# One PSUM bank set of five instead of 2 + 2 + 1 in a fused attention layer on one core

## Chip, cores and metric

The kernel runs on one core of a Trainium2 chip. The metric is the device time of one execution in microseconds (us). An execution of before takes 1867.32 us (median of three runs, 1866.57 to 1867.34).

## The reference

One encoder layer on x of shape (1, 2048, 1024), all float32: a modulated RMSNorm, one combined input projection, three groups of attention heads that share nothing but that projection, a gate for each, one output projection, a residual and a final RMSNorm. Cut to what matters:

```python
mod = c_act @ w_ada + b_ada
shift, scale, gate = jnp.split(mod, 3, axis=-1)
h = rmsnorm(x, norm_g) * (1.0 + scale[:, None, :]) + shift[:, None, :]
z = h @ w_in
...
a_out = mla_mixer(a_cq, a_ckv, a_kpe, ...)           # 6 heads, causal by chunks of 64
b_out = chunk_band_mixer(b_q, b_k, b_v, b_rel_bias)  # 5 heads, own chunk and 8 before, position bias
c_out = forgetting_mixer(c_q, c_k, c_v, c_f, ...)    # 5 heads, causal, cumulative log-forget bias
y = jnp.concatenate([a_out * silu(a_gate), b_out * silu(b_gate), c_out * silu(c_gate)], axis=-1) @ w_out
out = rmsnorm(x + gate[:, None, :] * y, final_g)
```

Each mixer is softmax(q k^T * scale + bias, masked) v for a head of 64 value columns.

## The kernel before

The 2048 tokens are worked off in two halves of 1024. Each half has a first stage (`stage_lv`: norm and transposition of x into `hT`, the latents of the A heads, the values of all heads, and the q and k of the first head) and then `attention()`, a loop over all 16 heads in a written order. In half 1 that order is B0 to B4, C0 to C4, A0 to A5. Every product of two float32 factors is made of three matmuls on rounded high and low parts (L359, L360, L361); a projection of one group of 128 columns for one block of 512 tokens is 24 such matmuls into one PSUM tile.

A head has two blocks of 512 queries, and a block is worked off in tiles of 128 keys by 512 queries, 580 score tiles in all. For a tile:
- TensorE makes the scores in a `st` tile (three or four matmuls, L982, L992 or L1050 to L1052).
- ScalarE takes exp of it three times (L755 into `ph`, L756 into `p32`, L758 in place), VectorE makes the low part `pl` (L764), GpSimd adds `p32` to the running sum (L769).
- Three tiles later TensorE adds the tile to `pv` by two matmuls (L778 with `ph`, L779 with `pl`).

At the end of a block ScalarE copies `pv` out (L784), GpSimd multiplies by the head's gate (L787, L788), and two tiles named `mx` turn the sums (L797, read by L798) and their reciprocals (L806, read by VectorE's L808, `oo`). Before a block can begin its queries need a row maximum: matmuls into `mx` tiles (L959, L970, L1040), reduced by VectorE (L962, L971, L1041), and a last turn by L722 to L723.

Between the tiles `step()` puts in a share of other work (`fill`): the projection of the next head's q and k into `pj` tiles (read by `evac`, ScalarE's L911, L912, L915, L916 and VectorE), the projections of the gates (G0 to G4, GA0 to GA2, read by ScalarE's L850 and VectorE's L851), and what the table `mids` lists by the head's number. In half 1 `mids[12]` loads the output weights (`load_wo`: DMA into one of three `wr` buffers, L1062; ScalarE's high part L1063; VectorE or GpSimd's low part L1064), `mids[13]` holds the last gate, GA2, and `mids[14]` and `mids[15]` the first eight of 16 output tiles (L1073 loads the heads' results into a `wr` buffer, L1076 and L1077 make `oh` and `ol`, then 48 matmuls into two `pj` tiles). The output weights `wo` take the one buffer of tag `big`, in which `hT` lies until its last reader, a matmul of GA2, has run.

PSUM has eight banks of 128 x 512 float32. Each PSUM tile is asked for by name through `pst(tag)`, and a tag has banks of its own: three for `st`, two for `mx`, two for `pj`, one for `pv`. Within a tag the banks are given out in the order in which the program asks. A tile that finds no free bank of its tag waits for the last reader of the oldest one. The order of the instructions on each engine is not that of the program text: a scheduler at build time places an instruction when its inputs and its buffer are free in its own reckoning, so the banks of a tag also set how far work may be placed ahead of its turn.

Of the kernel before, what the change touches and what calls it, by code (L numbers as in the profile page):

```python
# [8 lines left out]
F32 = mybir.dt.float32  # L9
# [52 lines left out]
def kernel(ctx: ExitStack, tc: tile.TileContext, a: dict, out: bass.AP):  # L62
# [8 lines left out]
    ps = ctx.enter_context(tc.tile_pool(name="ps", bufs=2, space=PSUM))  # L71
    dr = ctx.enter_context(tc.tile_pool(name="dr", bufs=1, space=DRAM))

    def pst(tag, bufs=2):
        return ps.tile([128, 512], F32, tag=tag, name=tag, bufs=bufs)

    def opool(name, bufs=2, side="left"):
        return tc.tile_pool(name=name, bufs=bufs, side=side, reuse_waits="tile")
# [100 lines left out]
    def h_units(hT, x_of, xn_of, tmp_of, ptag, norms=None):  # L179

        pairs = []
        for p2 in range(4):
            xns = []

            def norm(j, p2=p2, xns=xns):
                t = p2 * 2 + j
                xt, xn = x_of(t), xn_of()
                if norms is None:
                    r = col("xrr")
                    x_norm(xt, xn, r)  # L190
                else:
                    r = norms[:, t:t + 1]
                A.activation(xn, xt, AF.Copy, scale=r)
                xns.append(xn)

            def turn(k, p2=p2, xns=xns, box={}):
                o = 256 * (k % 2)
                if o == 0:
                    box["tp"] = pst(ptag, 3 if ptag == "st" else 2)
                tp = box["tp"][:, o:o + 256]  # L200
                for j in range(2):
                    T.transpose(tp[:, 128 * j:128 * j + 128], xns[j][:, 128 * k:128 * k + 128], ident)
                tmp = tmp_of(k)
                A.activation(tmp, tp, AF.Identity, scale=sc1[:, k:k + 1], bias=shf[:, k:k + 1])
                h = hT()
                hi = h[:, 0, k, 256 * p2:256 * p2 + 256]
                V.tensor_scalar(hi, tp, sc1[:, k:k + 1], shf[:, k:k + 1], op0=ALU.mult, op1=ALU.add)
                (V, G)[k % 2].tensor_tensor(h[:, 1, k, 256 * p2:256 * p2 + 256], tmp, hi.bitcast(F32), op=ALU.subtract)
            pairs.append([lambda j=j, f=norm: f(j) for j in range(2)] + [lambda k=k, f=turn: f(k) for k in range(8)])
# [12 lines left out]
    with opool("ada", 2, "right") as pool:  # L222

        mod = pst("mx")
        for c in range(2):
            acc = pool.tile([128, D], F32, tag="acc", name="acc")
            if c == 1:
                ident = load_const("ident", [128, 128])
                bada = load_const("b_ada", [128, 24])
                ng = load_const("norm_g", [128, 8])  # L230
                dma(out=posi, in_=a["positions"])
                dma(out=inv, in_=a["inv_freq"].to_broadcast([128, 16]))
                rotary(pool)
            for k in range(8):
                wa = pool.tile([128, D], F32, tag="wa", name="wa", bufs=8)
                dma(out=wa, in_=a["w_ada"][128 * k:128 * k + 128, D * c:D * c + D])
                if k == 0:
                    V.tensor_scalar(acc, wa, cact[:, 0:1], 0.0, op0=ALU.mult, op1=ALU.add)
                else:
                    V.scalar_tensor_tensor(acc, in0=wa, scalar=cact[:, k:k + 1], in1=acc, op0=ALU.mult, op1=ALU.add)  # L240
            for j in range(8):
                T.matmul(mod[:, 8 * c + j:8 * c + j + 1], lhsT=acc[:, 128 * j:128 * j + 128], rhs=ones[:, 0:1], start=True, stop=True)
        for u in h0[0][:2]:
            u()
        V.tensor_tensor(shf, mod[:, 0:8], bada[:, 0:8], op=ALU.add)
        V.tensor_tensor(sc1, mod[:, 8:16], bada[:, 8:16], op=ALU.add)
        V.scalar_tensor_tensor(sc1, in0=sc1, scalar=1.0, in1=ng, op0=ALU.add, op1=ALU.mult)
# [20 lines left out]
    def late_constants():  # L268
        tp = pst("mx")
        T.transpose(tp[:, 0:128], tri, ident)  # L270
        V.tensor_scalar(mtt, tp[:, 0:128], 1.0, BIG, op0=ALU.subtract, op1=ALU.mult)
# [1061 lines left out]
```

## Time and profile before

| what | value |
|---|---|
| median of three runs | 1867.32 us |
| the profiled execution, its own time | 1863.08 us |
| its span | 1861.1 us |
| mean granted TensorE clock | 0.983 of full speed |
| instructions | 28271 |
| TensorE busy | 1714.6 us (92%) |
| ScalarE busy | 1195.3 us (64%) |
| VectorE busy | 1132.8 us (61%) |
| GpSimd busy | 1071.9 us (58%) |

The profiled execution lies 4.2 us under the median of the runs, and its span 2.0 us under its own time. A busy time is the union of an engine's instructions; PE is the TensorE's matmuls, PEld its weight loads, DVE the VectorE, ACT the ScalarE, POOL GpSimd, SP the engine that issues the DMAs. A line as `PE pj L359 <- ACT q L916` reads: a matmul of line 359 into a tile named pj waited, and what came last was the ScalarE instruction of line 916 that writes q.

### The profile page before, as it was taken

Reading aid. Unit: us, or ns where it says so; the run is one execution under the profiler, and the core shown is the slowest. Engines: PE = TensorE matmul, PEld = TensorE weight load, DVE = VectorE, ACT = ScalarE, POOL = GpSimd, SP = SyncE. Lnnn points to the kernel's source line nnn. Section 1 sums busy time; section 2 is a strip of 40 time slices with the busy share of each in tenths; the row PEclk is TensorE's granted clock in tenths of the full one; section 3 lists DMA queues with packets and bytes.
Section 4 is the critical chain, followed back from the end, with each engine's and each line's share of the span. In section 5 each row is a group of like instructions: output and inputs, shape, how many; then the busy total and the mean of one; then the engine's idle time right before and its main releaser. Section 6 shows DMA issues by size and latency. Waiting matters only on the chain.

```text
span 1861.1 us, 28271 instructions
## 1 busy us (share of the span) xinstructions
PE 1714.6 (92%) x8835; PEld 1415.7 (76%) x8835; DVE 1132.8 (61%) x2447; ACT 1195.3 (64%) x2574; POOL 1071.9 (58%) x1256
## 2 busy tenths in 40 slices
PE   3899989999999986999899999999999997999997
PEld 2799868778777754999778887777777775877786
DVE  7453547866656587344456667777777776644322
ACT  3552347678768688342357778898998887665611
POOL 1541137568655557340156666777777778787864
PEclk9999989999999999999999999999999998999999
DMA  7514845435223241144933232222332334332243
GB/s 278 166 56 149 223 137 154 124 105 186 73 77 115 63 137 46 58 133 120 249 107 95 82 89 77 75 61 76 91 99 86 88 102 129 95 113 72 71 139 113
DMA packets 139994, 209.83 MB, mean 113 GB/s; under 512 B 18734, under 2 KB 72494, under 8 KB 139764
## 3 DMA queue, kind: packets, MB, share of 16 engines
q1 hardware_dynamic: 139844, 208.03, 37.2%
q8 instruction: 70, 1.15, 0.3%
q14 instruction: 80, 0.66, 0.1%
HBM read 154.05 MB, written 57.38 MB: 114 GB/s over the span
## 4 chain that ended last, share of the span: by engine, by line
PE 41%; ACT 7%; POOL 4%; issue 3%; DVE 3%; DMA 1%; SPq 0%; ACTq 0%; DVEq 0%; POOLq 0%
PE pj L359 5%; PE pj L360 5%; PE pj L361 5%; PE pv L778 3%; PE pv L779 3%; PE st L992 2%; PE st L982 2%; ACT st L758 1%; PE mx L1040 1%; PE mx L959 1%; ACT ph L755 1%; ACT p L756 1%; PE st L1051 1%; PE st L1052 1%; POOL p L769 1%
## 5 line engine op out<-in xcount | busy, mean ns | idle before, releaser
L769 POOL TENSOR_TENSOR p<-p,p 128x512 f32<-128x512 f32 (+3 forms) x516 | 539.7, 1046 | 248.8 <-ACT p L756 206.5
L764 DVE TENSOR_TENSOR pl<-st,ph 128x512 fp32r<-128x512 f32 (+1 forms) x580 | 332.7, 576 | 200.3 <-ACT st L758 191.7
L755 ACT ACTIVATE ph<-st 128x512 fp32r<-128x512 f32 (+1 forms) x580 | 299.3, 516 | 226.8 <-PE st L992 121.6
L758 ACT ACTIVATE st<-st 128x512 f32<-128x512 f32 (+1 forms) x580 | 303.8, 524 | 0.0
L756 ACT ACTIVATE p<-st 128x512 f32<-128x512 f32 (+1 forms) x580 | 297.5, 513 | 0.7
L359 PE MATMUL pj<-hT,whi 128*128 128x512 f32 x544 | 223.5, 411 | 14.0 <-ACT q L916 14.0
L779 PE MATMUL pv<-pl,v 128*128 128x512 f32 (+1 forms) x580 | 213.9, 369 | 22.8 <-DVE pl L764 22.5
L778 PE MATMUL pv<-ph,v 128*128 128x512 f32 (+1 forms) x580 | 215.5, 372 | 10.5 <-ACT ob L784 9.8
L360 PE MATMUL pj<-hT,whi 128*128 128x512 f32 x544 | 216.8, 399 | 0.0
L361 PE MATMUL pj<-hT,wlo 128*128 128x512 f32 x544 | 216.5, 398 | 0.0
L1041 DVE TENSOR_REDUCE pm<-mx 128x1 f32<-128x512 f32 (+2 forms) x240 | 139.7, 602 | 30.0 <-PE mx L1040 28.6
L779 PEld LDWEIGHTS pv<-pl,v 128*128 128x128 f32 x580 | 110.6, 191 | 51.7 <-DVE pl L764 37.2
L778 PEld LDWEIGHTS pv<-ph,v 128*128 128x128 f32 x580 | 110.9, 191 | 39.3 <-ACT ob L784 22.6
L962 DVE TENSOR_REDUCE pm<-mx 128x1 f32<-128x512 f32 (+2 forms) x200 | 116.5, 604 | 33.5 <-PE mx L959 16.3
L787 POOL TENSOR_TENSOR oa<-oa,ob 64x512 f32<-64x512 f32 x64 | 82.7, 1292 | 82.8 <-ACT oa L786 49.7
L359 PEld LDWEIGHTS pj<-hT,whi 128*128 128x128 f32 x544 | 104.4, 192 | 28.5 <-ACT q L916 14.8
L992 PE MATMUL st<-q,k 128*128 128x512 f32 (+1 forms) x340 | 124.1, 369 | 0.7 <-DVE q L723 0.7
L982 PE MATMUL st<-q,k 128*128 128x512 f32 (+1 forms) x340 | 119.7, 352 | 1.4 <-DVE pl L764 1.0
L361 PEld LDWEIGHTS pj<-hT,wlo 128*128 128x128 f32 x544 | 103.6, 190 | 21.6
L360 PEld LDWEIGHTS pj<-hT,whi 128*128 128x128 f32 x544 | 104.2, 192 | 15.8
L1040 PE MATMUL mx<-k,q 128*128 128x512 f32 (+2 forms) x240 | 85.5, 387 | 17.3 <-DVE oo L808 8.9
L359 PE MATMUL pj<-wo,oh 128*128 128x512 f32 x256 | 101.1, 395 | 0.0
(393 smaller groups left out, 4186.6 us busy)
## 6 DMA issues: line engine op xcount, KB each, us to landing
wr<-in_w_in SPq DMA_DIRECT2D x54, 512.0 KB
wr<-in_x SPq DMA_DIRECT2D x34, 512.0 KB
v<-dva SPq DMA_DIRECT2D x36, 256.0 KB
q<-dqa SPq DMA_DIRECT2D x48, 192.0 KB
k<-dka SPq DMA_DIRECT2D x72, 128.0 KB
wa<-in_w_ada SPq DMA_DIRECT2D x16, 512.0 KB
do<-oo SPq DMA_DIRECT2D x64, 128.0 KB
wr<-do SPq DMA_DIRECT2D x128, 64.0 KB
```

The costliest lines, as they stand in the source:

```text
L359: T.matmul(dst, lhsT=lh, rhs=rh, start=i == 0, stop=False)
L360: T.matmul(dst, lhsT=lh, rhs=rl, start=False, stop=False)
L361: T.matmul(dst, lhsT=ll, rhs=rh, start=False, stop=i == n - 1)
L755: A.activation(ph[:, v0:v1], st[:, v0:v1], AF.Exp, scale=scale)
L756: A.activation(p32[:, v0:v1], st[:, v0:v1], AF.Exp, scale=scale)
L758: A.activation(st[:, v0:v1], st[:, v0:v1], AF.Exp, scale=scale)
L764: V.tensor_tensor(pl[:, c0:c1], st[:, c0:c1], ph[:, c0:c1].bitcast(F32), op=ALU.subtract)
L769: G.tensor_tensor(acc[:, c0:c1], acc[:, c0:c1], p32[:, c0:c1], op=ALU.add)
L778: T.matmul(pv[:, c0:c1], lhsT=vt, rhs=ph[:, c0:c1], start=n == 0, stop=False)
L779: T.matmul(pv[:, c0:c1], lhsT=vt, rhs=pl[:, c0:c1], start=False, stop=n == len(js) - 1)
L982: T.matmul(st[:, c0:c1], lhsT=k2[:, ks], rhs=q2[:, c0:c1], start=True, stop=False)
L992: T.matmul(st[:, c0:c1], lhsT=k1[:, ks], rhs=q1[:, c0:c1], start=False, stop=True)
```

## The change

`pst` keeps the three banks of `st` under a tag of its own, and gives all other PSUM tiles (`mx`, `pj`, `pv`) one common tag with five banks. The sum stays eight banks.

```diff
     def pst(tag, bufs=2):
-        return ps.tile([128, 512], F32, tag=tag, name=tag, bufs=bufs)
+
+        share, bufs = ("st", 3) if tag == "st" else ("bank", 5)
+        return ps.tile([128, 512], F32, tag=share, name=tag, bufs=bufs)
```

The computation is the same, and so are the instructions, but for their order: the five banks are given out in the order in which the program asks for `mx`, `pj` and `pv` tiles together, and the scheduler places the instructions anew. The lines of the changed kernel lie two further down from here on (L359 becomes L361).

Start of the attention of half 0, on ScalarE. `q` and `k` are what `evac` takes out of the first head's two `pj` tiles, `teh` is its bias table, `whi` the high part of weights, `sg` the gate that is read out of a `pj` tile of group G0. Before:

```order
L349 ACTIVATE whi<-wr 128x1024
L915 ACTIVATE k_2672<-pj 64x512
L903 ACTIVATE teh<-te 128x256
L916 ACTIVATE q_2674<-pj 64x512
L915 ACTIVATE k_2686<-pj 64x512
L916 ACTIVATE q_2688<-pj 64x512
L903 ACTIVATE teh<-te 128x256
L850 ACT_TABLE_LOAD
L850 ACTIVATE sg<-pj 128x512
```

With the change:

```order
L351 ACTIVATE whi<-wr 128x1024
L917 ACTIVATE k_2672<-pj 64x512
L905 ACTIVATE teh<-te 128x256
L918 ACTIVATE q_2674<-pj 64x512
L917 ACTIVATE k_2686<-pj 64x512
L918 ACTIVATE q_2688<-pj 64x512
L852 ACT_TABLE_LOAD
L852 ACTIVATE sg<-pj 128x512
L905 ACTIVATE teh<-te 128x256
```

The first `sg` has moved ahead of the second `teh`; the four copies of the `pj` tiles stand as they did.

The last matmuls of GA2, the last readers of `hT`, on TensorE (`st` are scores of an A head, `pv` values). In before the last one, L361 of `hT,wlo`, stands where 495 of the 580 score tiles have been begun:

```order
L1050 MATMUL st<-q_17653,k_17553 128x256
L1051 MATMUL st<-q_17653,k_17552 128x256
L1052 MATMUL st<-q_17654,k_17552 128x256
L778 MATMUL pv<-ph,v 128x512
L360 MATMUL pj<-hT,whi 128x512
L361 MATMUL pj<-hT,wlo 128x512
L779 MATMUL pv<-pl,v 128x512
L1050 MATMUL st<-q_17653,k_17553 128x128
L1051 MATMUL st<-q_17653,k_17552 128x128
```

With the change the last one (L363 of `hT,wlo`) stands where 523 tiles have been begun, 28 score tiles later:

```order
L1052 MATMUL st<-q_17888,k_17843 128x256
L1053 MATMUL st<-q_17888,k_17842 128x256
L1054 MATMUL st<-q_17889,k_17842 128x256
L361 MATMUL pj<-hT,whi 128x512
L362 MATMUL pj<-hT,whi 128x512
L363 MATMUL pj<-hT,wlo 128x512
L724 MATMUL mx<-c_ident,mpad_251 128x128
L780 MATMUL pv<-ph,v 128x512
```

All 48 matmuls of GA2 moved: in before the first stands behind 446 score tiles begun, now behind 503.

The first matmul with the output weights, on TensorE. In before it stands behind 512 score tiles begun:

```order
L1050 MATMUL st<-q_17888,k_17673 128x512
L1051 MATMUL st<-q_17888,k_17672 128x512
L1052 MATMUL st<-q_17889,k_17672 128x512
L797 MATMUL mx<-c_ident,p_18286 128x128 x3
L1050 MATMUL st<-q_17888,k_17673 128x512
L1051 MATMUL st<-q_17888,k_17672 128x512
L1052 MATMUL st<-q_17889,k_17672 128x512
L797 MATMUL mx<-c_ident,p_18286 128x128
L359 MATMUL pj<-wo,oh 128x512
```

With the change it stands behind 530 tiles begun:

```order
L1052 MATMUL st<-q_18361,k_18318 128x512
L1053 MATMUL st<-q_18361,k_18317 128x512
L1054 MATMUL st<-q_18362,k_18317 128x512
L1052 MATMUL st<-q_18361,k_18318 128x512
L1053 MATMUL st<-q_18361,k_18317 128x512
L1054 MATMUL st<-q_18362,k_18317 128x512
L361 MATMUL pj<-wo,oh 128x512
```

Between the last reader of `hT` and the first reader of `wo` there were 112 other matmuls (44,672 columns in all), and there are 31 now (12,800 columns). On ScalarE the eight `wo` (L1063, now L1065) and the first `oh` (L1076, now L1078) moved along with them: the first `wo` stood among the exps of tile 495 and the first `oh` behind those of 507 tiles; now the first `wo` stands behind the exps of 523 tiles and the first two `oh` behind those of 527, directly after the last `wo`.

## Rows read from the trace of the kernel before

**Rows 1.** The page's busy times by engine: busy us, share of the span, instructions.

```profile
PE 1714.6 (92%) x8835; PEld 1415.7 (76%) x8835; DVE 1132.8 (61%) x2447; ACT 1195.3 (64%) x2574; POOL 1071.9 (58%) x1256
```

**Rows 2.** The page's chain that ended last, share of the span by engine.

```profile
PE 41%; ACT 7%; POOL 4%; issue 3%; DVE 3%; DMA 1%; SPq 0%; ACTq 0%; DVEq 0%; POOLq 0%
```

**Rows 3.** Waits of TensorE: idle us in total, times, longest.

```profile
PE pv L779 <- DVE pl L764: 22.5, 18, 4.9
PE pj L359 <- ACT q L916: 14.0, 2, 7.4
PE pv L778 <- ACT ob L784: 9.8, 21, 1.5
PE mx L1040 <- DVE oo L808: 8.9, 5, 2.4
PE mx L1040 <- DVE pm L1041: 7.4, 6, 2.3
...
PE mx L806 <- DVE pm L1041: 2.1, 1, 2.1
PE mx L970 <- DVE pm L971: 2.1, 5, 1.0
```

**Rows 4.** Stretches (window, length, busy us of each engine, granted clock, DMA).

```profile
247.84:252.00 4.16, 4.16 (x10) 3.29 (x11) 0.00 (x0) 1.15 (x2) 0.14 (x1) 0.50 0.49 147
252.00:260.00 8.00, 8.00 (x34) 6.53 (x33) 0.69 (x1) 2.30 (x3) 3.49 (x6) 0.92 0.71 229
...
930.47:936.00 5.53, 5.53 (x13) 4.37 (x14) 1.38 (x2) 1.74 (x3) 0.56 (x3) 0.51 0.98 244
936.00:944.00 8.00, 8.00 (x36) 6.59 (x36) 0.69 (x1) 0.91 (x2) 2.79 (x3) 1.00 0.53 164
1440.00:1526.00 86.00, 82.40 (x379) 65.16 (x379) 65.39 (x118) 73.82 (x159) 65.59 (x56) 0.98 0.28 79
1526.00:1567.40 41.40, 28.91 (x114) 20.50 (x113) 31.45 (x46) 31.06 (x61) 31.89 (x22) 0.84 0.50 152
...
1100.00:1400.00 300.00, 292.30 (x1411) 224.05 (x1410) 233.30 (x416) 266.22 (x561) 219.74 (x182) 1.00 0.28 80
...
936.00:1440.00 504.00, 488.98 (x2439) 387.80 (x2439) 364.02 (x758) 412.63 (x905) 344.66 (x304) 1.00 0.29 84
```

**Rows 5.** Timeline of TensorE at the start of half 0's attention: start, us, what.

```profile
239.78 0.39 PE L360 MATMUL pj<-hT,wbhi 128*128 128x512 f32 x1
240.00 0.39 PE L361 MATMUL pj<-hT,wblo 128*128 128x512 f32 x1
247.84 0.79 PE L359 MATMUL pj<-hT,whi 128*128 128x512 f32 x1 [7.45 <-ACT q L916]
```

**Rows 6.** The same at the start of half 1's attention.

```profile
930.47 0.79 PE L359 MATMUL pj<-hT,whi 128*128 128x512 f32 x1 [6.54 <-ACT q L916]
```

**Rows 7.** Timeline of ScalarE, half 0: G0's weights, then the first head's copies.

```profile
234.07 1.05 ACT L349 ACTIVATE whi<-wr 128x1024 fp32r<-128x1024 f32 x1
...
242.59 0.59 ACT L915 ACTIVATE k<-pj 64x512 fp32r<-64x512 f32 x1
246.75 0.42 ACT L903 ACTIVATE teh<-te 128x256 fp32r<-128x256 f32 x1 [3.57 <-POOL te L900]
247.20 0.59 ACT L916 ACTIVATE q<-pj 64x512 fp32r<-64x512 f32 x1
```

**Rows 8.** Lines of 1525 to 1569: durations min/median/max in ns, first and last start.

```profile
L1063 ACT ACTIVATE wo<-wr x8: 1038/1057/1062, 1526.3 to 1544.3; 128x1024 fp32r<-128x1024 f32 x8
...
L1064 DVE TENSOR_TENSOR wo<-wr,wo x4: 1225/1779/5193, 1527.4 to 1546.3; 128x1024 fp32r<-128x1024 f32 x4
...
L1073 SPq DMA_DIRECT2D wr<-do x16: 378/430/531, 1547.0 to 1555.2; - x16
```

**Rows 9.** Timelines of TensorE and ScalarE: GA2's last matmul, first `oh`, its first reader.

```profile
1525.83 0.39 PE L361 MATMUL pj<-hT,wlo 128*128 128x512 f32 x1
...
1562.68 1.11 ACT L1076 ACTIVATE oh<-wr 128x1024 fp32r<-128x1024 f32 x1
...
1567.39 0.47 PE L359 MATMUL pj<-wo,oh 128*128 128x512 f32 x1
```

## The prediction, made before the changed kernel was run

> **What bounds the kernel.** I read the busy times by engine first: TensorE is busy 92% of the span, no other engine over 64% [rows 1]. Then the chain that ended last: TensorE's matmuls hold 41% of it, ScalarE 7% [rows 2]. So the time is TensorE's work plus the moments in which TensorE stands still, 1861.1 - 1714.6 = 146.5 us; the same matmuls run after the change, so it can win only idle time and time at the low clock. Third, TensorE's waits [rows 3], to sort the idle time by what was missing. A wait of an mx, pj or pv matmul for the reader of an older tile of its tag is a wait for a bank: pj behind L916 (14.0 us, two waits), pv behind `ob` (9.8, 21 waits), mx behind `oo` (8.9) and behind `pm` (7.4 + 2.1 + 2.1). The largest other row, pv behind `pl` (22.5 us), is one for data, and more banks do nothing for it. Fourth, stretches of the span [rows 4]: in 1100 to 1400 TensorE is busy 292 of 300 us and ScalarE 266, so there ScalarE is next in line. A difference of 0.2% (3.7 us) is about what a measurement of this kernel can tell from none.
>
> **Term 1: the two starts of the attention.** At 240.4 TensorE has finished the first head's two projections and wants to begin G0. Both pj banks hold the first head's tiles, and their last reader L916 stands on ScalarE behind `teh`, which waits 3.57 us for GpSimd's bias table; G0's first matmul comes 7.45 us late [rows 5, 7]. G0's weights were ready long before (L349 at 234.07) [rows 7]. The same happens at 930.47, 6.54 us [rows 6]. In the new order G0 takes another bank of the five, whose last reader belongs to the stage before; the order on ScalarE agrees, since the first `sg` moves ahead of a `teh`. So I count both waits as gone: 7.45 + 6.54 = 14.0. After each, the granted clock is 0.50 and 0.51, the 1.2 GHz level, while before it matmuls ran 0.22 us apart [rows 4, 5]. From 247.84 to 260 there are 44 matmuls in 12.16 us; at 0.228 us each (between the 0.22 and the 0.235 of 34 in 8 us) they need 10.0. From 930.47 to 944 there are 49 in 13.53 us, which need 11.2. That is 2.1 + 2.4 = 4.5 us more. Term 1: **-18.5**. What is late next are the first head's maxima, which need the copies L911 to L916 and the bias; they are done by about 248.4, and G0's 48 matmuls (10.9 us) last until about 251.5, so they cover that. If the head start were lost again there (the bias is waited for in any case), the term is 0; if not, it cannot exceed 19.
>
> **Term 2: the short bank waits.** Rows 3 without L916 give 9.8 + 8.9 + 7.4 + 2.1 + 2.1 = 30.3 us in 35 waits, each adding about 0.1 us for a longer first matmul: 34 us. Some 8 us of it lie in the stretch of term 3 and are counted there, so 26 are left. Which go? In the order I looked for how many matmul columns stand between the last matmul into a bank's old tile and the first into its new one. At 0.228 us per 512 columns, reuses within 2 us fall from 417 to 170, within 1.2 us from 170 to 57. So about 60 to 67% of the tight ones go: I take two thirds, -17.5. A freed wait can become one for data: the pv matmul behind `pl` stands closer to its scores in a few dozen tiles more (under 2.5 us in 37 of 580 instead of 17). At 22.5 us for 18 waits, 1.25 us each [rows 3], of which perhaps four more appear, that is +4.5. Term 2: **-13**; bounds 0 (every wait moves to `pl` or to ScalarE) and -26.
>
> The Trainium skill says of such gaps, on its page "Perfetto Trace Analysis", section "Optimization Strategy", that the same gap repeating on the engine that should be saturated can mean that there isn't enough SBUF or PSUM for the next tile. Rows 3 agree for the 35 short waits, and by that alone all of the 26 us would go and the sum would be -34.5, some 1833 us. The 22.5 us behind `pl` show that not all gaps here are of that kind.
>
> **Term 3: the output weights come late.** `wo` takes the buffer of `hT`, so `load_wo` can't begin before GA2's last matmul. In before, the two-bank pj tag let GA2 run ahead of its turn, at 495 tiles begun; in the common tag it gets its bank in program order, at 523. The output tiles don't move back with it: their first matmul stands at 530 instead of 512. In before the way from GA2's last matmul to the first with `wo` took from 1525.83 to 1567.39, 41.6 us [rows 9]; TensorE was busy 28.9 us of it, at a clock of 0.84 [rows 4], thus idle 12.5. Now it has 31 matmuls, 12,800 columns, 5.7 us, and then nothing but to wait for `oh`. How long is the chain? As it ran: `oh` ended at 1562.68 + 1.11, 38.0 us after GA2 [rows 9]. As short as I can make it from the rows: the eight conversions L1063 run from 1526.3 to 1545.4 and are paced by three `wr` buffers; the last low part on VectorE took 5.19 us where the quickest took 1.23 (-4); the first eight L1073 take from 1547.0 some 4 us to issue, and between the last landing and `oh` ScalarE had exps to do (-3 or so) [rows 8]; ScalarE interleaved exps with L1063 throughout (-5): 26. So TensorE idles 20 to 32 us there. I take 24, nearer to the short end, since ScalarE has little else to do once the scores stop: +11.5 against before. Besides, with GA2 gone from 1440 to 1526, ScalarE bounds that stretch (73.8 of 86 us busy [rows 4]): TensorE's idle time grows from 3.6 to about 6 us, +2.5. Against it, the stretch between (tiles 495 to 523) gets 48 matmuls more and has little idle time and a full clock: the 0.84 of before cost 0.16 x 28.9 = 4.6 us. Clock after the new stop: +2.4, as in term 1. 11.5 + 2.5 - 4.6 + 2.4, rounded down for the bank waits of that stretch which go too: **+10**; bounds -2 and +22.
>
> **Sum.** -18.5 - 13 + 10 = -21.5 on the profiled execution's 1863.1 us, 1841.6. The median of the runs lies 4.2 us above that execution; I give the number against the median: 1867.3 - 21.5 = 1845.8, say **1845**. Everything else (the start up to 230 us, the last eight output tiles) keeps its order or has no bank waits, and I cost it at nothing.
>
> **Rivals.**
> - *Larger gain.* The chain of `wo` is short (26 us), all bank waits go and none turn to `pl`: -18.5 - 26 + 0 = -44, 1823. For it: TensorE has 92% busy and would still be at only 94%. Against: ScalarE at 266 of 300 us [rows 4].
> - *No change.* Freed banks let TensorE issue earlier, but in 936 to 1440 it is already busy 489 of 504 us at full clock [rows 4], and the tiles come at ScalarE's pace; term 2 is 0, and term 1 is half lost to the maxima (-9), term 3 gives +10: 1868. The Trainium skill's page "Perfetto Trace Analysis", section "Matmul Optimizations", asks only that all eight PSUM banks be used. Before used eight as well; by that rule nothing is to be had here, and no row bears it out: the waits of rows 3 happen with eight in use.
> - *Slower.* The late `wo`: the chain is as long as before, 38 us to `oh`, TensorE stands for 32 of them, and that is +22 with the clock; if the short waits only halve and turn to `pl` (-13 + 8), and the head start is half lost (-9), the sum is +8, 1875. It decides from a stop of 24 + 21.5 = 45 us if terms 1 and 2 are as I have them, and from about 28 us if they bring only 14. For it: the three `wr` buffers pace the chain whatever else runs [rows 8]. Against: before shared ScalarE and VectorE with exps during it, and 45 us is above my bound.
> - *The change doesn't do what it says.* The scheduler's reckoning isn't the chip; the first G0 matmul could find its bank's reader late as well. Then term 1 is 0: 1864.
>
> **Chances.** My forecast (1830 to 1862) 0.62, larger gain 0.13, no change 0.11, slower 0.11, not as said 0.03. The range reaches from the larger gain's 1823 to where the slower case begins: 1824 to 1869. Faster by over 0.2% (under 1863.6): 0.77; within 0.2%: 0.11; slower (over 1871): 0.12.
>
> **What would show it.** Term 1: the wait of L361 behind L918 is gone from TensorE's waits, no idle stretch over 2 us at the two starts, the clock near 1.0 there. Term 2: pv behind `ob`, mx behind `oo` and `pm` sum to about 12 us instead of 30, with pv behind `pl` at 25 to 30. Term 3: one stop of TensorE of 20 to 32 us some 6 us behind GA2's last matmul, ended by `oh` (L1078) or `wo` (L1065), and a low clock behind it. The forecast is wrong if that stop is over 40 us or missing, if the first G0 matmul still waits, or if the waits behind `pl` or for ScalarE grow by over 15 us.

## The result

The changed kernel is slower: 1881.89 us (median of four runs, 1880.49 to 1883.04) against 1866.94 us of before in the same session, a ratio of 1.0091 with a 95% interval of 1.0078 to 1.0103. The forecast was 1845 us and faster.

The page of the changed kernel, its busy times and its chain:

```profile
span 1878.3 us, 28274 instructions
PE 1726.9 (92%) x8835; PEld 1435.8 (76%) x8835; DVE 1131.2 (60%) x2447; ACT 1196.8 (64%) x2574; POOL 1073.5 (57%) x1256
PE 38%; ACT 6%; POOL 5%; issue 4%; DVE 4%; DMA 1%; SPq 0%; DVEq 0%; POOLq 0%; ACTq 0%
```

Beside [rows 1] the reader sees where the 17.2 us of span went. TensorE's idle time grew from 146.5 to 1878.3 - 1726.9 = 151.4 us, by 4.9 only. Its busy time grew by 12.3 us, with the same 8,835 matmuls, while the mean granted clock fell from 0.983 to 0.968.

TensorE's waits in the changed kernel (idle us in total, times, longest):

```profile
PE pv L781 <- DVE pl L766: 29.3, 28, 3.2
...
PE mx L724 <- DVE mpad L720: 12.3, 12, 5.4
PE st L1052 <- DVE pl L766: 7.7, 5, 3.4
PE st L984 <- DVE mpad L720: 7.3, 4, 2.4
PE pj L361 <- ACT oh L1078: 6.9, 1, 6.9
PE mx L1042 <- DVE pm L1043: 4.7, 5, 2.0
...
PE mx L972 <- DVE pm L973: 3.1, 5, 0.9
...
PE mx L972 <- DVE sg L853: 3.0, 1, 3.0
...
PE pj L361 <- ACT q L918: 1.0, 2, 0.6
```

Against [rows 3]: most of the waits for a bank did go. The pj wait behind the copy of q fell from 14.0 to 1.0 us, pv behind `ob` from 9.8 to none, mx behind `pm` and `oo` from 20.5 to 7.8. One is new: a maximum whose mx tile takes the bank of a gate waits 3.0 us for `sg`. In place of the others stand waits of the row turn for VectorE's `mpad` (the row maxima, 12.3 us; 3.3 in before), of scores that the profile puts down to `mpad` (7.3 us), waits for `pl`, and one for `oh`.

**Where on the way.** The starts of the first exp of each score tile (L755, in the changed kernel L757) on ScalarE's timeline are milestones that all these programs pass in the same order. The table gives them in before's profiled execution, and how far the others are behind it (plus) or ahead (minus), in us. Below the changed kernel stand ten runs of the next section. Each row is one execution. The 17 executions of before in one session lie between 1857.84 and 1867.93 us, so a step of a few us in a single row shows nothing by itself.

| score tile | 12 | 108 | 156 | 191 | 204 | 492 | 528 | 579 |
|---|---|---|---|---|---|---|---|---|
| before, start | 289.7 | 517.5 | 656.8 | 737.9 | 969.1 | 1523.1 | 1601.6 | 1757.6 |
| changed kernel | -4.5 | -3.7 | +10.1 | +19.8 | +14.4 | +9.8 | +19.1 | +15.6 |
| pj_own | +0.2 | -0.8 | -0.5 | +2.7 | 0.0 | +0.4 | -4.7 | -4.8 |
| pv_own | -3.9 | +4.4 | +9.3 | +10.8 | +7.9 | +7.0 | -0.8 | +7.4 |
| mx_own | -6.1 | -5.1 | -5.7 | -5.2 | -12.9 | -16.6 | -6.2 | -10.4 |
| pj3 | -2.8 | -0.6 | +1.4 | +6.9 | -1.6 | +26.3 | +11.0 | +10.9 |
| after_ga2_early | -5.0 | -4.3 | +9.9 | +18.7 | +13.6 | +14.1 | +9.0 | +7.5 |
| after_teh | -10.7 | -7.4 | +4.9 | +13.8 | +5.2 | +0.8 | +10.1 | +6.6 |
| before_fill_mx | +1.4 | +1.5 | +8.5 | +11.0 | +8.8 | +12.0 | +10.9 | +10.8 |
| row_own | -2.6 | +4.4 | +7.6 | +7.7 | +1.2 | +2.7 | +13.3 | +13.3 |
| row_st | -6.1 | -9.6 | -9.4 | -7.1 | -11.9 | -8.8 | +1.6 | -0.5 |
| mx_own_ga2_teh | -11.2 | -10.8 | -11.4 | -10.4 | -20.4 | -15.6 | -24.8 | -24.8 |

The changed kernel wins 4.5 us at the first start, loses 23.5 us between tiles 108 and 191 (the end of half 0) and wins 5.4 us at the second start. Its steps on either side of tile 492 can't be read one by one, because GA2's matmuls moved across that tile. Tiles 204 to 492 and 492 to 528 as two stretches, in before, in the changed kernel and in after_ga2_early, a run of the next section that puts GA2 ahead of tile 492 again (window, length, busy us of PE, PEld, DVE, ACT, POOL with the number of instructions, granted clock, DMA):

```profile
969.15:1523.10 553.95, 537.16 (x2646) 425.31 (x2645) 407.79 (x814) 465.51 (x1011) 390.77 (x338) 1.00 0.29 82
1523.10:1601.56 78.46, 64.23 (x270) 48.70 (x269) 59.26 (x94) 62.19 (x126) 62.59 (x46) 0.89 0.48 141
```

```profile
983.52:1532.87 549.35, 527.93 (x2601) 419.33 (x2600) 406.67 (x816) 464.60 (x1010) 390.59 (x338) 0.99 0.29 83
1532.87:1620.69 87.82, 72.82 (x317) 57.30 (x316) 57.66 (x95) 63.42 (x128) 63.37 (x47) 0.86 0.43 127
```

```profile
982.77:1537.19 554.42, 536.72 (x2655) 428.69 (x2653) 410.96 (x820) 469.01 (x1015) 392.52 (x338) 1.00 0.29 84
1537.19:1610.57 73.38, 62.36 (x259) 48.07 (x260) 52.18 (x90) 59.10 (x122) 61.27 (x47) 0.91 0.50 141
```

The changed kernel has 45 matmuls fewer ahead of tile 492 and 47 more behind it. From tile 204 to 528 the three take 632.4, 637.2 and 627.8 us: without the late gate the changed kernel is 4.6 us faster there than before, and the late gate costs 9.4 us.

**The end of half 0.** Two stretches of it, before and then the changed kernel (columns as above):

```profile
517.48:656.80 139.32, 138.63 (x709) 108.07 (x708) 83.53 (x158) 98.21 (x207) 71.86 (x62) 1.00 0.29 86
656.80:737.86 81.06, 61.89 (x323) 44.97 (x322) 71.26 (x142) 70.14 (x155) 52.70 (x54) 0.98 0.33 97
```

```profile
513.75:666.88 153.13, 144.36 (x709) 112.94 (x708) 83.31 (x158) 98.80 (x207) 71.76 (x62) 0.96 0.26 78
666.88:757.69 90.81, 71.40 (x323) 53.77 (x323) 73.16 (x143) 70.98 (x155) 54.46 (x56) 0.83 0.29 86
```

In the first stretch 709 matmuls take 5.7 us longer at clock 0.96 and 8.1 us more are idle. In the second the idle time is nearly the same (19.2 and 19.4 us), and of the 9.8 us more 9.5 are busy time of the same 323 matmuls, at a clock of 0.83 instead of 0.98.

TensorE of the changed kernel at score tile 114, the end of a block, with VectorE's instructions that it waited for:

```profile
522.28 0.44 PE L984 MATMUL st<-q,k 128*128 128x512 f32 x1
525.06 0.47 PE L984 MATMUL st<-q,k 128*128 128x512 f32 x1 [2.33 <-DVE mpad L720]
525.37 0.27 PE L724 MATMUL mx<-c_ident,mpad 128*128 128x128 f32 x1
525.39 0.48 PE L780 MATMUL pv<-ph,v 128*128 128x512 f32 x1
...
523.89 0.69 DVE L964 TENSOR_REDUCE pm<-mx 128x1 f32<-128x512 f32 x1
524.50 0.41 DVE L766 TENSOR_TENSOR pl<-st,ph 128x256 fp32r<-128x256 f32 x1
524.83 0.15 DVE L720 TENSOR_REDUCE mpad<-pm 128x4 fp32r<-128x8 f32 x1
```

The score that starts at 525.06 comes out of the stop. The profile names `mpad`; in the program this score (st_6319 below) waits for the `pl` just ahead of it on VectorE, which frees its `st` bank. The two end 0.07 us apart, and the row turn behind waits for `mpad`.

In before the same place reads (a projection's matmuls run while VectorE works off the maxima):

```profile
526.36 0.30 PE L992 MATMUL st<-q,k 128*128 128x128 f32 x1
526.50 0.45 PE L359 MATMUL pj<-hT,whi 128*128 128x512 f32 x1
...
528.84 0.27 PE L722 MATMUL mx<-c_ident,mpad 128*128 128x128 f32 x1
```

TensorE's order in the changed kernel says why nothing filled the gap. A tile's number tells when the program asked for it:

```
L984 MATMUL st_6298<-q2_6108,k2_5933 128x512
L984 MATMUL st_6319<-q2_6108,k2_5933 128x512
L724 MATMUL mx_6253<-c_ident_134,mpad1_252 128x128
L780 MATMUL pv_6259<-ph_6132,v_5945 128x512
L781 MATMUL pv_6259<-pl_6166,v_5945 128x512
L799 MATMUL mx_6271<-c_ident_134,p32_5904 128x128 x4
L361 MATMUL pj_6280<-hT_89,whi_6136 128x512
```

The row turn mx_6253 can run only when VectorE has reduced the last maximum. It was asked for before pv_6259 and pj_6280, so in one queue of banks the block's values and the next projection stand behind it. In before the eight value matmuls of this place are spread over the scores of tiles 112 to 114, with a projection's matmuls between them; here all eight come behind the row turn, which stands behind the scores of tile 114. The same pattern stands at tiles 138, 150, 162 and 186.

**The output weights.** TensorE of the changed kernel, from GA2's last matmul to the first with `wo`:

```profile
1584.68 0.39 PE L363 MATMUL pj<-hT,wlo 128*128 128x512 f32 x1
...
1591.73 0.48 PE L781 MATMUL pv<-pl,v 128*128 128x128 f32 x1 [2.98 <-DVE pl L766]
...
1599.52 0.80 PE L1052 MATMUL st<-q,k 96*128 96x512 f32 x1 [3.37 <-DVE pl L766]
1608.11 0.80 PE L361 MATMUL pj<-wo,oh 128*128 128x512 f32 x1 [6.93 <-ACT oh L1078]
```

The same way as a stretch (columns as above):

```profile
1584.60:1608.10 23.50, 10.02 (x34) 6.70 (x32) 12.09 (x14) 16.38 (x27) 18.41 (x11) 0.63 0.71 219
```

The way took 23.4 us, not 41.6 [rows 9]. TensorE was idle 13.5 us of it and ran the rest at clock 0.63.

**The starts.** G0 no longer waits, but the row turn does, for work that stands behind a bias table on ScalarE. ScalarE, VectorE and TensorE of the changed kernel, half 0:

```profile
254.26 0.42 ACT L905 ACTIVATE teh<-te 128x256 fp32r<-128x256 f32 x1 [4.40 <-POOL te L902]
...
255.53 0.58 ACT L852 ACTIVATE sg<-pj 128x512 f32<-128x512 f32 x1
...
256.13 0.69 DVE L853 SCALAR_TENSOR_TENSOR sg<-sg,pj 128x512 f32<-128x512 f32 x1 [4.39 <-ACT sg L852]
...
257.74 0.48 PE L724 MATMUL mx<-c_ident,mpad 128*128 128x128 f32 x1 [5.36 <-DVE mpad L720]
```

The second head's bias table (`teh`) waits 4.40 us for GpSimd, the second gate `sg` stands behind it on ScalarE, VectorE finishes that gate and only then the last maximum.

### The profile page after: what moved, and what is told of

Its sections match the earlier page's. It is cut to its first block, busy times and chain, and to the rows that moved or that the text cites. A ratio compares the mean times of both kernels' runs of the same rounds, so it can differ in the third digit from the quotient of the medians.

```text
span 1878.3 us, 28274 instructions
## 1 busy us (share of the span) xinstructions
PE 1726.9 (92%) x8835; PEld 1435.8 (76%) x8835; DVE 1131.2 (60%) x2447; ACT 1196.8 (64%) x2574; POOL 1073.5 (57%) x1256
## 4 chain that ended last, share of the span: by engine, by line
PE 38%; ACT 6%; POOL 5%; issue 4%; DVE 4%; DMA 1%; SPq 0%; DVEq 0%; POOLq 0%; ACTq 0%
PE pj L361 6%; PE pj L363 6%; PE pj L362 6%; PE pv L781 3%; PE pv L780 2%; PE st L994 2%; POOL p L771 2%; ACT st L760 2%; PE st L984 1%; DVE pl L766 1%; ACT p L758 1%; ACT ph L757 1%; PE mx L961 1%; PE mx L1042 1%; PE st L1054 1%
## 5 line engine op out<-in xcount | busy, mean ns | idle before, releaser
L757 ACT ACTIVATE ph<-st 128x512 fp32r<-128x512 f32 (+1 forms) x580 | 298.9, 515 | 239.2 <-PE st L994 119.6
L781 PE MATMUL pv<-pl,v 128*128 128x512 f32 (+1 forms) x580 | 218.1, 376 | 30.3 <-DVE pl L766 29.3
L361 PE MATMUL pj<-hT,whi 128*128 128x512 f32 x544 | 226.4, 416 | 1.7 <-ACT q L918 1.0
L363 PE MATMUL pj<-hT,wlo 128*128 128x512 f32 x544 | 216.9, 399 | 0.0
L1043 DVE TENSOR_REDUCE pm<-mx 128x1 f32<-128x512 f32 (+2 forms) x240 | 137.7, 601 | 36.9 <-PE mx L1042 35.7
L964 DVE TENSOR_REDUCE pm<-mx 128x1 f32<-128x512 f32 (+2 forms) x200 | 114.7, 602 | 30.0 <-PE mx L961 17.0
L780 PEld LDWEIGHTS pv<-ph,v 128*128 128x128 f32 x580 | 113.5, 196 | 18.7 <-issue 1.4
L363 PEld LDWEIGHTS pj<-hT,wlo 128*128 128x128 f32 x544 | 104.4, 192 | 23.4
L361 PEld LDWEIGHTS pj<-hT,whi 128*128 128x128 f32 x544 | 105.5, 194 | 16.3 <-ACT q L918 1.3
L361 PE MATMUL pj<-wo,oh 128*128 128x512 f32 x256 | 102.5, 400 | 6.9 <-ACT oh L1078 6.9
L363 PE MATMUL pj<-wo,ol 128*128 128x512 f32 x256 | 101.2, 395 | 1.2 <-POOL ol L1079 1.2
```

The lines of the kernel that those rows point to most:

```text
L361: T.matmul(dst, lhsT=lh, rhs=rh, start=i == 0, stop=False)
L363: T.matmul(dst, lhsT=ll, rhs=rh, start=False, stop=i == n - 1)
L757: A.activation(ph[:, v0:v1], st[:, v0:v1], AF.Exp, scale=scale)
L780: T.matmul(pv[:, c0:c1], lhsT=vt, rhs=ph[:, c0:c1], start=n == 0, stop=False)
L781: T.matmul(pv[:, c0:c1], lhsT=vt, rhs=pl[:, c0:c1], start=False, stop=n == len(js) - 1)
```

## The experiments

Theory A was that the projections lose their own queue of banks. B: freed bank waits turn into waits for data, whoever shares. C: pv's sharing is what hurts. The first four runs share in other ways. They differ from before in `pst` alone, here the line of each run:

```diff
-        return ps.tile([128, 512], F32, tag=tag, name=tag, bufs=bufs)
+        share, bufs = {'st': ('st', 3), 'pj': ('pj', 2), 'mx': ('bank', 3), 'pv': ('bank', 3)}[tag]    # pj_own
+        share, bufs = {'st': ('st', 3), 'pv': ('pv', 1), 'mx': ('bank', 4), 'pj': ('bank', 4)}[tag]    # pv_own
+        share, bufs = {'st': ('st', 3), 'mx': ('mx', 2), 'pj': ('bank', 3), 'pv': ('bank', 3)}[tag]    # mx_own
+        share, bufs = {'st': ('st', 3), 'pj': ('pj', 3), 'mx': ('bank', 2), 'pv': ('bank', 2)}[tag]    # pj3
+        return ps.tile([128, 512], F32, tag=share, name=tag, bufs=bufs)
```

> pj gets its two banks back, mx and pv share three, st keeps three. Theory A (the loss comes from the projections: in a common set they get their banks in program order, so they cannot run ahead of their turn, fill no gap at the ends of the blocks of half 0, and let the last gate and with it the output weights come late): the projections stand as in before, the stops of over 2 us in half 0 and the stop at the output weights are gone, 1860 to 1867 us. Theory B (freed bank waits turn into waits for data on VectorE and ScalarE, whoever shares): the values no longer have to wait for the copy of pv here either, so the loss stays, 1877 or more. Theory C (pv sharing its bank is what hurts): loss stays as well, 1877 or more.

> pv gets its one bank back, mx and pj share four, st keeps three. Theory A: the last gate comes late and the projections of half 0 stand as in the changed kernel, so the time is that of the changed kernel within 5 us, 1877 to 1887. Theory B: between the two, about 1875. Theory C: as before, 1863 to 1869.

> mx gets its two banks back, pj and pv share three, st keeps three. The order has the projections of half 0 as in before, but the last gate late, from 501 to 523 tiles begun. Theory A: the end of half 0 is as in before (no stop over 2 us at tiles 114, 138, 150), the stop at the output weights is there and costs 5 to 10 us: 1870 to 1877. Theory B: loss in both halves, 1877 or more. Theory C: loss in both halves, 1877 or more.

> pj gets three banks of its own, mx and pv share two, st keeps three. Theory A: the projections run further ahead than in before (the last gate ends at 455 tiles begun instead of 495), the first gate projection of each half finds a free bank, so the stops of 7.45 and 6.54 us and the low clock after them go or move to the next waiting instruction; mx and pv with two banks in place of three wait more, some 10 us. 1853 to 1868. Theory B and C: mx and pv in a common set of two cost more than in any other kernel, 1885 or more.

| run | median us | ratio to before | 95% interval |
|---|---|---|---|
| pj_own | 1858.33 | 0.9966 | 0.9952 to 0.9979 |
| pv_own | 1874.19 | 1.0052 | 1.0037 to 1.0067 |
| mx_own | 1855.31 | 0.9951 | 0.9937 to 0.9965 |
| pj3 | 1876.26 | 1.0069 | 1.0054 to 1.0083 |

B and C in their simple form fall: pv shares in pj_own and mx_own, and both are faster than before. What loses is pj in one set with mx (pv_own and the changed kernel), and mx and pv in a set of two (pj3). A was wrong on sizes: pj_own came out at the lower edge of its range (below it in us, 1860.6 by its ratio), pv_own below its range, where B had put it (about 1875), mx_own far below (its last gate runs late too, and it still wins). pj3 lost where a gain was expected: 27.9 us between tiles 204 and 492, of which 15.3 came back up to tile 528. With two banks for mx and pv its waits of mx L1041 behind `pm` are 14.5 us (7.4 in before). In mx_own the end of half 0 costs nothing (-5.1 to -5.2); what its late gate costs, mx_own_ga2 below shows.

**The late gate, the bias table, the filling projections.** Four runs took the places one by one.

```diff
-                mid = {1: "G1", 3: "G2", 5: "G3", 7: "G4", 9: "GA0", 10: "GA1", 13: "GA2"}
+                mid = {1: "G1", 3: "G2", 5: "G3", 7: "G4", 9: "GA0", 10: "GA1", 12: "GA2"}    # after_ga2_early, mx_own_ga2
```

```diff
-            A.activation(teh[:, 0:256], te, AF.Copy)
+            G.tensor_scalar(teh[:, 0:256], te, 1.0, 0.0, op0=ALU.mult, op1=ALU.add)    # after_teh
```

```diff
-            box["p"] = pst("pj")
+            box["p"] = pst(tag)    # before_fill_mx: "mx" for G3, G4, GA2 of half 0 and block 1 of QC1, QC3, QC4, else "pj"
```

> The changed kernel with the last gate of half 1 put one head earlier in the table (its 48 matmuls at tiles 473 to 486 instead of 503 to 523, the first matmul with the output weights behind 526 tiles begun). Theory A (projections that queue behind mx in one set, told by place: ends of the blocks in half 0, the late output weights in half 1, a jam behind the bias table at the starts): only the stop at the output weights goes, 6 to 11 us less than the changed kernel (1881.9 against 1866.9 of before, ratio to before 1.002 to 1.006), half 0 as it was. Theory D (the loss is one of chance patterns of short stops and the low clock after them, all over): no steady gain, ratio 1.007 or more.

> The changed kernel with the bias table's high part (teh) made by GpSimd instead of ScalarE, so that no copy and no gate on ScalarE stands behind it. Theory A: the stops of 5.36 us (half 0) and 2.96 + 1.60 us (half 1) at the starts go, with the low clock behind them 8 to 14 us less than the changed kernel, ratio to before 1.001 to 1.005; at score tile 12 it is 9 to 12 us ahead of before instead of 4.5. Rival E (the maxima or the first scores wait for something else that is as late): the ratio stays at 1.007 or more.

> The kernel before, but nine projection tiles near the end of half 0 (gates G3, G4, GA2 and the second projections of heads C1, C3, C4) take their bank from mx (two banks) instead of pj, so that they begin at 114, 138 and 150 tiles begun instead of 112, 136 and 148; nothing else changes its place. Theory A: at each of the three places TensorE stops for 2 us or more and the clock falls, 4 to 6 us each, ratio to before 1.006 to 1.011. Theory D or a loss that comes from pv or from the number of banks: within 0.2% of before.

> mx with two banks of its own, pj and pv three together, and the last gate of half 1 one head earlier. Theory A: the gain of that set at the starts and the ends of blocks stays, the stop at the output weights (10 us between tiles 516 and 528) goes: 5 to 10 us less than the run with mx alone (ratio 0.9951), ratio 0.990 to 0.993. Theory D: ratio 0.995 as without it.

| run | median us | ratio to before | 95% interval |
|---|---|---|---|
| after_ga2_early | 1872.82 | 1.0043 | 1.0027 to 1.006 |
| after_teh | 1871.84 | 1.0042 | 1.0028 to 1.0055 |
| before_fill_mx | 1873.07 | 1.0045 | 1.0031 to 1.0059 |
| mx_own_ga2 | 1846.35 | 0.9900 | 0.9884 to 0.9916 |

The late gate costs the changed kernel 0.0048 (9 us), and the bias table 0.0049 (9 us); both are as expected, and D and E fall with them. mx_own wins 0.0051 (9.5 us) by the early gate, also as expected. In after_teh the stop of 5.36 us at the row turn became this one:

```profile
253.76 0.33 PE L724 MATMUL mx<-c_ident,mpad 128*128 128x128 f32 x1 [1.15 <-DVE mpad L720]
```

before_fill_mx loses less than expected: 2.4 to 2.7 us at each of the tiles 114, 138 and 150, where the changed kernel loses 4.1, 3.9 and 5.4. So projections that come late are a part of that loss. No low clock followed there (1.00 from tile 108 to 156), and the values, which it leaves in their own bank, were not held up.

**The head of the queue.** That left theory F: the row turn stands ahead of the values as well as of the projections. The first test gave it a bank of its own.

```diff
-        share, bufs = ("st", 3) if tag == "st" else ("bank", 5)
+        share, bufs = {"st": ("st", 3), "row": ("row", 1)}.get(tag, ("bank", 4))
...
-            tp = pst("mx")
+            tp = pst("row")    # in m_rows, put()
```

> The changed kernel, but the tile of the row turn (L722 of before, L724 of the changed kernel) gets one bank of its own, and the common set has four. Nothing else is edited. Theory F (in one set the row turn, which waits for VectorE's last maximum, stands ahead of the next block's values and of the next projection, so that both stand still until it has its bank): the values at the ends of blocks are spread again in the order, the stops of 2.3 us at score tiles 114, 138 and 150 and the low clock of tiles 156 to 191 are gone or halved; of the 23.5 us lost between tiles 108 and 191 at most 10 are left, ratio to before 0.999 to 1.005. Theory C (values that share banks with projections and maxima lose, whatever stands first): loss as in the changed kernel, 1.007 or more.

Measured: 1878.39 us, ratio 1.0082 (1.0065 to 1.01). The total missed its range, as C would have it, but the place did what F says: between tiles 108 and 191 it loses 3.3 us instead of 23.5. The gain is given back before tile 108 (8.1 us behind the changed kernel there) and behind tile 204; that four common banks instead of five are the reason was not shown. So this run couldn't decide, and a second one took the row turn's bank from `st` and left the common set at five.

```diff
-            tp = pst("mx")
+            tp = pst("st")    # in m_rows, put(); pst as in the changed kernel
```

> The changed kernel with one edit: the tile of the row turn takes its bank from the three of st, so that the common set of five keeps its number and loses only this one kind of tile. Theory F (the row turn, which waits for VectorE's last maximum, stands at the head of the common queue and holds up values and projections): the value matmuls stand spread at the ends of the blocks, most of the 23.5 us between tiles 108 and 191 is gone (at most 8 left) while the gain of the starts stays; the stop at the output weights stays (+9); ratio to before 0.994 to 1.000. Theory G (the region is lost because banks, whatever their number, are shared by all three kinds): the loss stays, 1.006 or more.

Measured: 1866.28 us, ratio 1.0011 (1.0002 to 1.002), a hair above the range of F and 15 us below the changed kernel. Between tiles 108 and 191 it loses 2.5 us. In its order two value matmuls and ten matmuls of the projection stand ahead of the row turn, which comes behind the scores of tile 111 instead of 114. The same two stretches as above, in row_st:

```profile
507.90:647.40 139.50, 137.88 (x710) 108.39 (x708) 82.98 (x159) 98.31 (x207) 71.90 (x62) 1.00 0.29 85
647.40:730.80 83.40, 66.77 (x322) 50.15 (x323) 68.77 (x142) 70.91 (x156) 54.17 (x56) 0.89 0.32 94
```

and its waits for `oh` at the output weights, which stay as they were, and at the row turn, 12.3 us in the changed kernel:

```profile
PE pj L361 <- ACT oh L1078: 6.9, 1, 6.9
...
PE st L724 <- DVE mpad L720: 2.1, 6, 0.8
```

G falls: all three kinds of tile still share five banks. F is shown for this stretch.

**All together.** Three runs join the undoings (the edits are those above).

> The three undoings together on the changed kernel: a bank of its own for the row turn, the last gate one head earlier, the bias table's high part on GpSimd. If the three places are separate and hold the whole loss, the gains add up: 1.0091 less 0.005 to 0.010, less 0.005, less 0.005, ratio 0.989 to 0.994. If they overlap, 0.995 or more.

> The same with the last gate one head earlier and the bias table's high part on GpSimd. If the three causes are separate and hold the whole loss: 0.0049 + 0.0049 below the run without these two, 0.984 to 0.990, level with the set of mx alone and pj with pv (0.9868). If a set of five costs otherwise: 0.992 or more.

> mx with two banks of its own, pj and pv three together, the last gate one head earlier, and the bias table's high part made by GpSimd. If the jam behind the bias table at the starts costs there as it did in the changed kernel, 4 to 9 us less than without that edit (ratio 0.990): 0.985 to 0.988. If the maxima are as late for another reason: 0.990.

| run | median us | ratio to before | 95% interval |
|---|---|---|---|
| row_own_ga2_teh | 1860.48 | 0.9982 | 0.9971 to 0.9993 |
| row_st_ga2_teh | 1839.13 | 0.9867 | 0.9851 to 0.9883 |
| mx_own_ga2_teh | 1838.56 | 0.9868 | 0.9849 to 0.9887 |

row_own_ga2_teh missed its range because row_own alone brought 0.0009 instead of 0.005 to 0.010; the other two gains add up to it (1.0082 - 0.0048 - 0.0049 = 0.9985). In row_st_ga2_teh the three edits together turn 1.0091 into 0.9867. The early gate and the bias table bring 0.0144 there (1.0011 to 0.9867), where they brought 0.0048 and 0.0049 in the changed kernel, so the causes are not fully separate. mx_own_ga2_teh is within its range; the bias table brings 0.0032 there. Both kernels beat before by 24.6 us in their sessions; between the two there is no difference that the runs can tell.

## Why the prediction was wrong

**The step that failed** is the last sentence of the sum: everything else "keeps its order or has no bank waits, and I cost it at nothing". None of the three terms has a cost at the end of half 0, so it fell to that sentence, and its order did change: the values and the projections went behind the row turn. It cost 23.5 us, more than the whole forecast gain; with the row turn out of the common set (row_st) 2.5 us of it are left. I had counted for every bank how far its reuses lie apart, but not what stands at the head of one common queue: a tile that is granted late holds up all that was asked for behind it. I used that rule for GA2 (term 3), and did not ask it of the values.

**Term 1** (-18.5) was right on the wait and wrong on what is late next. The waits of 7.45 and 6.54 us are gone; by tiles 12 and 204 they brought 4.5 and 5.4 us. "They cover that" failed: the second `sg` stands behind the second `teh`, the instruction with which the order that I showed ends; I looked at the first `sg` only. With `teh` moved (after_teh) the two gains are 10.7 and 8.6 us, 19.3, a hair over the bound of 19 that I gave.

**Term 2** (-13). The bank waits of [rows 3] (38 of them, not 35) fell from 30.3 to 4.7 + 3.1 = 7.8 us in the rows that answer to them; with mx behind `sg` (3.0) and behind `s` (2.2) it is 13.0, near the 12 that I named as the sign. But 4.5 us (5.0, had I multiplied rightly) was far too little for what takes their place: `pl` from 22.5 to 29.3, the row turn and the scores put down to `mpad` 16.3 more (12.3 + 7.3 against 3.3), A's scores behind `pl` from 2.5 to 7.7. Much of that lies at the starts and at the end of half 0. Away from the three places the changed kernel gained 4.6 us (tiles 204 to 528 by after_ga2_early) and 3.5 us (tiles 528 to 579) and lost 0.8 us (tiles 12 to 108), 7.3 us in all.

**Term 3** (+10) came out at 9 us by the medians of after_ga2_early and at 9.4 us by its stretches. The mechanism was right; that the sum fits is luck, since its parts don't. The way to `oh` was shorter than I could make it (23.4 us to the first matmul), and TensorE was idle 13.5 us of it, not 24. Against after_ga2_early the idle time grows by 3.7 us up to tile 492 and by 4.0 us from there to 528, and the busy time by 1.7 us.

**The rivals.** The slower one named the late output weights as the cause. They are a part, but the stop that it needed (28 us at least) wasn't reached: 13.5 us were idle. The kernel became slower through a place that no rival named. The reading of the Trainium skill's page "Perfetto Trace Analysis", section "Optimization Strategy" (repeated gaps can mean too little PSUM), by which the sum would have been 1833 us, holds for the bank waits that went, and not for the time: the trace has other gaps in their place, and the idle time as a whole grew by 4.9 us. By the section "Matmul Optimizations" of the same page of the Trainium skill nothing was to be had, since eight banks were in use. The runs differ: the five kernels that differ from before in `pst` alone all use eight banks, and lie between 0.9951 and 1.0091 of its time. How the banks are shared decides.

**What stays open.** In the second stretch (tiles 156 to 191) before and the changed kernel are idle alike, and only the clock differs. row_st took most of that loss away (2.3 us are left of 9.7), so the held-up queue brings it about; why these stops lower the clock there and those of before hardly do was not settled.

## What to carry to other kernels

Before several kinds of buffers are put in one set, ask of each which of them waits longest before it can use its bank, and what was asked for behind it: in a set that is granted in program order, that one sets the pace of all. Sharing pays where no kind waits long for another engine (pj with pv here), and the kind that waits keeps banks of its own. A static count of how far reuses lie apart says nothing of this; read the order at the ends of blocks for runs of work that used to be spread.

## What the runs showed of the hardware

Over the whole span the low clock cost more than the added idle time: TensorE's idle time grew by 4.9 us, and the same matmuls took 12.3 us longer, at a mean clock of 0.968 instead of 0.983. And the length of a stop alone doesn't tell whether the clock falls. At 525.06 the changed kernel comes out of a stop of 2.33 us (shown above); before has one of the same length, again behind VectorE:

```profile
704.98 0.50 PE L1040 MATMUL mx<-k,q 128*128 128x512 f32 x1 [2.34 <-DVE pm L1041]
```

The five us from that instruction on, in the changed kernel and in before:

```profile
525.06:530.06 5.00, 5.00 (x18) 4.09 (x19) 1.86 (x4) 0.65 (x4) 1.62 (x2) 0.66 0.14 53
```

```profile
704.98:710.00 5.02, 3.75 (x17) 2.37 (x17) 5.02 (x10) 3.76 (x9) 3.78 (x4) 1.00 0.12 26
```

One ran at 0.66, though TensorE was busy all the time, the other at full clock, with a quarter of it idle.
